# A hybrid decoder trunk on one core: eight row tiles instead of four in seven-product form for the first pair of the first MLP product in two of its four groups

## The chip, the cores and the metric

One core of a Trainium2 chip runs the whole program. The metric is the device time of one execution in microseconds; the runs of the kernel before gave 1497.21 to 1497.78 us, with a median of 1497.4 us over three. All inputs and the output are float32. Names of engines are those of the profile: PE multiplies matrices (PEld loads its weights), DVE is the vector engine, ACT the scalar engine, POOL the engine for general work, SP the engine that only issues transfers here.

## What is computed

One decoder layer on 256 tokens with 2048 channels, and 16 meta tokens ahead of them: two attention branches, gates, an output projection, and then the part that matters here, a squared-ReLU MLP with 8192 hidden channels:

```python
h = h + hybrid_mixer(rmsnorm(h, norm_mix_g[l]), ...)
h = h + squared_relu_mlp(rmsnorm(h, norm_mlp_g[l]), w_ff1[l], w_ff2[l])
return rmsnorm(h, final_norm_g)[:, N_META:]

def squared_relu_mlp(xn, w1, w2):
    return jnp.square(jax.nn.relu(xn @ w1)) @ w2
```

## The kernel before, in words

**Float32 in three products.** A float32 product is made of three products of rounded halves. Every weight tile comes from DRAM into one of five `raw` buffers (SP issues the load), ACT copies it rounded into the high half of a `w` buffer, and DVE writes the rest, `raw - high`, into the low half (`cut`, lines 967 to 975). There are five `w` buffers, too. `product_into` (line 984) then multiplies, for two row tiles: high by high, high by low, low by high, so six matmuls of 512 columns for a product, all on line 993.

**Seven products for eight.** For a pair of column blocks (`f1`, `f2 = f1 + 4`) and the two halves of the tokens, four row tiles can be taken as 2 x 2 blocks in a form with seven products instead of eight (`pair_of`, lines 998 to 1114). The form needs differences of weight tiles (`less`, on DVE, line 977) and sums of token tiles (`summed`, from the tiles given as `sums`). The steps `m1` to `m7` are its products, `held` loads the two tiles of `f2` into buffers of their own (`hb`, `hc` for the first four row tiles, `hd`, `he` for the next four; `he` lies in a tile whose name in the trace is `sums`). Row tiles outside the form are taken plainly (`plain`): one cut for twelve matmuls. `pair_of` gets a list `sums`; its length `nq` says how many fours of row tiles take the form. With `nq == 1` the form has eight steps, 42 matmuls and 7 cuts, 4 differences, and twelve plain steps follow (`rest`). With `nq == 2` it has sixteen steps, 84 matmuls, 14 cuts, 8 differences, and eight plain steps follow; the tile of `f1` then stays in its `raw` buffer, is overwritten there with a difference (`got["a", q]`), and one tile of `f2` is loaded a second time (`m3`).

**The MLP.** The 8192 hidden channels are taken in four groups (`NG`). A group has four pairs: two of the first product (operand `x2`), two of the second (operand `a`, made by `hidden` from the first product's results). The loop over `coming` (lines 1363 to 1393) runs the plain steps of one pair and puts the first steps of the next pair between them; the tables `at` say after which plain step each goes. This document calls the four rounds of that loop in a group stage 0 to stage 3: in stage 3 the plain steps of the second product's second pair run, between the first steps of the next group's first pair. Only the second pair of the second product had `nq == 2`, with the sums tiles `s_a` and `s_x2`.

**The sums of x2.** The token sums of `x2`'s first four row tiles are made in the output projection (`token_sums`, line 907 ff., out of `gained`, line 1267), stay in `s_x2`, are stored to DRAM (`kept_sums`, line 1279) and are loaded again by four transfers on POOL's queue in stage 3 of each group (line 1378), since `s_x2` holds sums of `a` in between.

**What sets the order.** Each engine runs its instructions in one fixed order, which a scheduler makes from the program's order and the dependences; PE's order may mix the matmuls of several steps.

Of the kernel before, what the change touches and what calls it, by code (L numbers as in the profile page):

```python
# [7 lines left out]
F32 = mybir.dt.float32  # L8
# [4 lines left out]
ALU = mybir.AluOpType  # L13
# [3 lines left out]
P = 128  # L17
# [3 lines left out]
NT = 256  # L21
# [10 lines left out]
RAW = 5  # L32
NL = 4
SUMS_AT = 24
SX_AT = 0
PARTS_AT = 56

# [36 lines left out]
def trunk(ctx: ExitStack, tc: tile.TileContext, hT, w_small, w_all, consts, w_alpha2, out):  # L74
    nc = tc.nc
    serial = [0]

    def nm(s):
        serial[0] += 1
        return f"{s}_{serial[0]}"  # L80
# [5 lines left out]
    dram = ctx.enter_context(tc.tile_pool(name="dram", bufs=1, space=bass.MemoryType.DRAM))  # L86
# [93 lines left out]
    def gemm2(w, x, k0=0, nk=KT, pool=None, last=None):  # L180

        ps = bank(pool or pg, "ps")
        for k in range(nk):
            hi, lo = w(k0 + k)
            if last is None or k < nk - 1:
                mac2(ps, hi, lo, x[:, k], k == 0, k == nk - 1)
            else:
                nc.tensor.matmul(steps(ps), hi, steps(row(x[:, k])), start=False, stop=False)
                nc.tensor.matmul(steps(ps[:, 0:NT]), lo, steps(last), start=False, stop=True)
        issued()  # L190
        return ps
# [51 lines left out]
    def total(ps, t=None):  # L243

        b = tmp.tile([P, NT], F32, tag="evb", name=nm("evb"), bufs=1)
        nc.scalar.copy(b, ps[:, NT:512])
        if t is None:
            t = sums4[:, NT * (turns[0] % 4) : NT * (turns[0] % 4 + 1)]
            turns[0] += 1
        nc.vector.tensor_tensor(t, ps[:, 0:NT], b, op=ALU.add)  # L250
        return t

    def split_to(dst_hi, dst_lo, src):
        nc.scalar.copy(dst_hi, src)
        nc.vector.tensor_tensor(dst_lo, src, dst_hi.bitcast(F32), op=ALU.subtract)
# [44 lines left out]
    def operand(pool, name, nk=KT, at=0, **kw):  # L300

        t = pool.tile([P, at + nk * 2 * NT], F32R, name=nm(name), **kw)
        return t[:, at:].rearrange("p (k o t) -> p k o t", o=2, t=NT)
# [33 lines left out]
    def gain(i, k):  # L337
        return residual[0][:, k, NA + i : NA + i + 1]
# [59 lines left out]
    for s in range(KT // 2):  # L398
# [5 lines left out]
        for kk in range(2):  # L404
            k = 2 * s + kk
# [496 lines left out]
    def token_sums(dst, src, temp):  # L902

        v = temp.rearrange("p (s k m) -> p s k m", s=4, m=P)
        c, d = (v[:, i].rearrange("p k (c r) -> p k c r", r=32) for i in (0, 1))
        s3, s4 = (v[:, i].rearrange("p k (c r) -> p k c r", r=32) for i in (2, 3))
        nc.vector.tensor_tensor(c, src(0, 1), src(1, 1), op=ALU.add)
        nc.vector.tensor_tensor(s3, src(0, 0), src(0, 1), op=ALU.subtract)
        nc.vector.tensor_tensor(d, c, src(0, 0), op=ALU.subtract)
        nc.vector.tensor_tensor(s4, src(1, 0), d, op=ALU.subtract)  # L910
        split_to(dst[:, :, :, 0, :], dst[:, :, :, 1, :], v)
# [13 lines left out]
    for t in range(2):  # L925
        nc.sync.dma_start(line1[:, P * t : P * t + P], rbt[0:1, P * t : P * t + P])
        nc.sync.dma_start(r1[:, t : t + 1], line1[:, P * t : P * t + P].rearrange("o p -> p o"))
    s_x = keep.tile([P, 32 * P + 64], F32R, tag="h", name="s_x")[:, SX_AT : SX_AT + 32 * P].rearrange(
        "p (q s k o m) -> p q s k o m", q=2, k=2, o=2, m=P)
# [245 lines left out]
    for j0 in (12, 14):  # L1175
# [4 lines left out]
        for j in range(2):  # L1180
            t = total(gemm2(w, of, k0=8 * j, nk=8))
            nc.vector.tensor_tensor(gates[2 * j], gates[2 * j], t, op=ALU.mult)
        for j in range(2):
            t = total(gemm2(next_weights(), og))
# [13 lines left out]
    ht = residual[0][:, :, NM:NA]  # L1198
    x2 = operand(keep, "x2", at=24, tag="s2")
# [18 lines left out]
    def turn_tile():  # L1218
        return gat.tile([P, KT * P], F32, tag="o", name=nm("turn"))

    def sums_tile(name):
        t = fp.tile([P, 16 * P + 64], F32R, name=name)
        return t[:, SUMS_AT : SUMS_AT + 16 * P].rearrange("p (s k o m) -> p s k o m", k=2, o=2, m=P)

    s_x2, s_a = sums_tile("s_x2"), sums_tile("s_a")
    gained = turn_tile()
    kept = dram.tile([P, KT * NT], F32, name="kept")
    kept_sums = dram.tile([P, 16 * P], F32, name="kept_sums").rearrange("p (s k o m) -> p s k o m", k=2, o=2, m=P)

    a_box = {}  # L1230

# [5 lines left out]
    def pairs():  # L1237
        for g in range(NG):
            for p in range(2):
                yield (g, p), lambda: pair_of(blocks(), x2, [s_x2], lambda f, pt, g=g, p=p: hidden(  # L1240
                    operand_a(g), 2 * p + f, pt, None if p else s_a if f == 0 else s_x2 if g < NG - 1 else None,
                    (g, p, f) == (NG - 1, 1, 1)), p == 0)
            for p in range(1 if g == NG - 1 else 2):
                yield None, lambda: pair_of(blocks(), operand_a(g), [s_a, s_x2] if p else [s_a], lambda f, pt, g=g, p=p: gathered(g, 2 * p + f, pt), p == 0, p == 0)
# [5 lines left out]
    def blocks():  # L1250
        ff[0] += 8
        return ff[0] - 8
# [7 lines left out]
    for j in range(KT):  # L1260
        add_residual(j, gemm2(next_weights(out=True), y))
        nc.scalar.activation(x2[:, j, 0, :], ht[:, j, :], AF.Identity, scale=gain(1, j))
        nc.vector.scalar_tensor_tensor(x2[:, j, 1, :], ht[:, j, :], gain(1, j),
                                       x2[:, j, 0, :].bitcast(F32), op0=ALU.mult, op1=ALU.subtract)
        square_sum(acc2, j, j == 0)
        if j < 4:
            nc.vector.tensor_scalar(gained[:, NT * j : NT * (j + 1)], ht[:, j, :], gain(1, j), None, op0=ALU.mult)
        if j == 3:
            g4 = gained[:, 0 : 4 * NT].rearrange("p (j t c r) -> p j t c r", j=4, t=2, r=32)
            token_sums(s_x2, lambda i, t: g4[:, 2 * i : 2 * i + 2, t], gained[:, 4 * NT :])  # L1270
        if j == 3:
            tc.keep_in_program_order(nc.scalar.preload_act_table_set("natural_log_exp_and_others"))
            steps_now, rest_now = first_pair[1]()
        if j in (3, 5, 8, 11):
            for step in {3: slice(0, 1), 5: slice(1, 3), 8: slice(3, 5), 11: slice(5, 7)}[j], :
                for run in steps_now[step]:
                    run()
        if j == 8:
            nc.scalar.dma_start(kept_sums, s_x2.bitcast(F32))
        if j % 4 == 3:  # L1280
            nc.scalar.dma_start(kept[:, NT * (j - 3) : NT * (j + 1)].rearrange("p (j t) -> p j t", t=NT),
                                ht[:, j - 3 : j + 1, :])
# [25 lines left out]
    def hidden(a, b, pt, sums, last):  # L1308

        both = turn_tile()  # L1310
        u = both[:, 4 * NT :].rearrange("p (t f) -> p t f", t=2)

        def part(t):
            nc.scalar.activation(u[:, t, :], pt[t], AF.Relu, scale=r2[:, t : t + 1])
            nc.scalar.activation(u[:, t, :], u[:, t, :], AF.Square)
            return cells(u[:, t, :])

        def ready(back):
            turned_parts(a, b, back)
            if b == 0:  # L1320
                summed(back)
            elif sums is not None:
                behind.append([2, lambda: summed(back)])

        def summed(back):
            token_sums(sums, lambda i, t: back[:, 2 * i : 2 * i + 2, t], both[:, 0 : 8 * P])

        turn([lambda t=t: part(t) for t in range(2)], ready, both, slots=(6, 9, 11) if last else (7, 11, 14 if b == 0 else 15))
# [34 lines left out]
    index, late = 0, []  # L1363
    while rest_now:
        key, make = next(coming, (None, None))
        steps_next, rest_next = make() if make else ([], [])
        at = {1: (0, 3, 4, 5, 6, 8, 9, 10), 2: (0, 2, 1, 2, 4, 5, 5, 6, 7, 7, 8, 8, 9, 9, 10, 11),
              3: (0, 2, 4, 5, 5, 6, 6, 7)}.get(index % 4, (0, 2, 3, 4, 5, 7, 9, 10))
        if index == 0:
            steps_now[7]()  # L1370
        closing = index == 4 * NG - 3
        for i, run in enumerate(rest_now):
            run()
            if index == 0 and i == 2:
                norm2()
            if index % 4 == 3 and i == 0:
                for q in range(4):
                    nc.gpsimd.dma_start(s_x2[:, q].bitcast(F32), kept_sums[:, q])
            for n, step in enumerate(steps_next):
                if at[n] == i and closing and n > 4:  # L1380
                    late.append(step)
                elif at[n] == i:
                    step()
            if not steps_next and i in (1, 3, 5):
                late.pop(0)()
        issued()
        rest_now, index = rest_next, index + 1
# [169 lines left out]
```

## Time and profile before

| | before |
|---|---|
| runs, median (lowest to highest) | 1497.4 us (1497.21 to 1497.78), three runs |
| the profiled execution | 1497.08 us; its span, first to last instruction, 1495.1 us; granted clock 0.999 |
| PE busy | 1484.9 us, 99% of the span |
| DVE busy | 1193.2 us, 80% |
| ACT busy | 878.4 us, 59% |
| POOL busy | 119.8 us, 8% |
| moved by DMA | 335.00 MB, 224 GB/s over the span |
| PE's share of the chain that ended last | 96% |

PE is busy from one end to the other; what DVE, ACT and the transfers do lies beside it. The share of DVE is a mean over stages: in some of them it has far less room than 80% says, and a reader should look at each stage by itself.

### The profile page before, as it was taken

What the parts mean: (1) busy time and instruction counts of PE and PEld (TensorE: products, weight loads), DVE (VectorE), ACT (ScalarE), POOL (GpSimd) and SP (SyncE); (2) the same over time, 40 slices, a digit from 0 to 9 for tenths busy, and PEclk for the clock granted to TensorE, in tenths of its full rate; (3) what the DMA queues carried; (4) which work ended last, traced back from release to release, by engine and by line L of the source; (5) the groups of instructions that cost most, each with busy time, mean ns of one, the idle gap of its engine ahead of it and who ended that gap; (6) DMA issues with size and microseconds to landing.
All of it is one profiled execution on the core that took longest, in us unless ns stands there. A gap on an engine that the chain in (4) does not pass through costs nothing.

```text
span 1495.1 us, 22541 instructions
## 1 busy us (share of the span) xinstructions
PE 1484.9 (99%) x8374; PEld 1322.2 (88%) x8374; DVE 1193.2 (80%) x1578; ACT 878.4 (59%) x1246; POOL 119.8 (8%) x202
## 2 busy tenths in 40 slices
PE   9999999999999999999999999999999999999997
PEld 8999999999999888888988888888888888888887
DVE  7899858586677877876788889877998889898766
ACT  7765444455555555555566666666665566556645
POOL 6012100111111000000011100000000000000004
PEclk9999999999999999999999999999999999999999
DMA  9545555465547677678678678877777778888783
GB/s 325 176 145 185 182 170 180 159 213 170 169 163 247 212 224 233 205 230 286 223 248 253 204 248 264 267 230 242 250 244 249 230 250 252 266 260 273 249 277 110
DMA packets 242545, 335.00 MB, mean 224 GB/s; under 512 B 13130, under 2 KB 209748, under 8 KB 242180
## 3 DMA queue, kind: packets, MB, share of 16 engines
q1 hardware_dynamic: 219940, 299.22, 61.2%
q10 hardware_dynamic: 21360, 30.09, 6.5%
q0 software_dynamic: 1136, 4.27, 0.9%
q8 instruction: 65, 1.06, 0.3%
q14 instruction: 44, 0.36, 0.1%
HBM read 316.22 MB, written 17.31 MB: 223 GB/s over the span
## 4 chain that ended last, share of the span: by engine, by line
PE 96%; DVE 2%; issue 1%; ACT 1%; POOL 0%; POOLq 0%; DVEq 0%; ACTq 0%
PE bx L993 17%; PE ps L169 14%; PE bv L993 11%; PE by L993 11%; PE bz L993 11%; PE ps L170 7%; PE psa L174 5%; PE psa L178 5%; PE psa L176 4%; PE gla L993 4%; PE fox L993 2%; PE ps L429 1%; PE ps L431 1%; PE ps L1424 1%; DVE w L135 1%
## 5 line engine op out<-in xcount | busy, mean ns | idle before, releaser
L973 DVE TENSOR_TENSOR w<-raw,w 128x1024 fp32r<-128x1024 f32 x300 | 365.4, 1224 | 100.9 <-ACT w L972 96.6
L972 ACT CAST w<-raw 128x1024 fp32r<-128x1024 f32 x300 | 312.3, 1048 | 203.6 <-PE bx L993 68.2
L135 DVE TENSOR_TENSOR w<-raw,w 128x1024 fp32r<-128x1024 f32 x198 | 243.0, 1229 | 81.5 <-ACT w L134 80.1
L134 ACT CAST w<-raw 128x1024 fp32r<-128x1024 f32 x198 | 207.4, 1049 | 92.4 <-PE psa L178 30.3
L169 PE MATMUL ps<-x,w 128*128 128x512 f32 x543 | 184.4, 383 | 0.0
L174 PE MATMUL psa<-x,w 128*128 128x272 f32 x640 | 181.7, 285 | 0.0
L178 PE MATMUL psa<-x,w 128*128 128x272 f32 x640 | 179.6, 282 | 0.0
L176 PE MATMUL psa<-x,w 128*128 128x272 f32 x624 | 175.9, 282 | 0.0
L170 PE MATMUL ps<-x,w 128*128 128x256 f32 x543 | 149.0, 274 | 0.0
L993 PE MATMUL bx<-w,x 128*128 128x512 f32 x528 | 131.1, 381 | 0.0
L174 PEld LDWEIGHTS psa<-x,w 128*128 128x128 f32 x640 | 120.2, 188 | 0.2
L178 PEld LDWEIGHTS psa<-x,w 128*128 128x128 f32 x640 | 120.2, 188 | 0.1
L176 PEld LDWEIGHTS psa<-x,w 128*128 128x128 f32 x624 | 117.4, 188 | 0.0
L169 PEld LDWEIGHTS ps<-x,w 128*128 128x128 f32 x543 | 101.9, 188 | 17.1
L993 PEld LDWEIGHTS bx<-w,x 128*128 128x128 f32 x528 | 98.8, 188 | 17.4
L993 PE MATMUL by<-w,x 128*128 128x512 f32 x444 | 112.5, 381 | 0.0
L170 PEld LDWEIGHTS ps<-x,w 128*128 128x128 f32 x543 | 102.0, 188 | 0.0
L993 PEld LDWEIGHTS by<-w,x 128*128 128x128 f32 x444 | 83.2, 188 | 14.6
L993 PE MATMUL bv<-w,x 128*128 128x512 f32 x360 | 91.9, 381 | 0.0
L993 PE MATMUL bz<-w,x 128*128 128x512 f32 x360 | 91.6, 381 | 0.0
L169 PE MATMUL ps<-y,w 128*128 128x512 f32 x256 | 85.6, 380 | 0.0
L993 PE MATMUL bx<-w,a 128*128 128x512 f32 x336 | 83.7, 380 | 0.0
(405 smaller groups left out, 2741.1 us busy)
## 6 DMA issues: line engine op xcount, KB each, us to landing
raw<-w_all_dram SPq DMA_DIRECT2D x489, 512.0 KB, 4.6
there<-turn ACTq DMA_DIRECT2D x80, 128.0 KB, 3.9
turn<-there ACTq DMA_DIRECT2D x20, 512.0 KB, 4.7
hb<-w_all_dram SPq DMA_DIRECT2D x18, 512.0 KB, 4.4
hc<-w_all_dram SPq DMA_DIRECT2D x18, 512.0 KB, 5.3
raw<-w_all_dram SPq DMA_DIRECT2D x26, 256.0 KB, 5.0
raw<-w_all_dram SPq DMA_DIRECT2D x8, 384.0 KB, 6.8
hd<-w_all_dram SPq DMA_DIRECT2D x6, 512.0 KB, 7.1
```

The costliest lines, as they stand in the source:

```text
L134: copied = nc.scalar.copy(hi[:, k, :], r).ins
L135: return copied, nc.vector.tensor_tensor(lo[:, k, :], r, hi[:, k, :].bitcast(F32), op=ALU.subtract).ins
L169: nc.tensor.matmul(steps(ps), hi, steps(row(x)), start=first, stop=False)
L170: nc.tensor.matmul(steps(ps[:, 0:NT]), lo, steps(x[:, 0, :]), start=False, stop=last)
L174: nc.tensor.matmul(steps(ps[:, X_LO]), hi, steps(x_lo[:, k]), start=first, stop=False, skip_group_check=True)
L176: nc.tensor.matmul(steps(ps[:, 0:NA]), lo, steps(x_hi[:, k]), start=False, stop=last and hi is None, skip_group_check=True)
L178: nc.tensor.matmul(steps(ps[:, 0:NA]), hi, steps(x_hi[:, k]), start=False, stop=last, skip_group_check=True)
L429: nc.tensor.matmul(steps(ps), hi, steps(row(x[:, k])), start=st, stop=False)
L431: nc.tensor.matmul(steps(ps[:, 0:NT]), lo, steps(x[:, k, 0]), start=False, stop=sp)
L972: copied = nc.scalar.copy(hi, r).ins
L973: made(copied, nc.vector.tensor_tensor(lo, r, hi.bitcast(F32), op=ALU.subtract).ins, 1)
L993: nc.tensor.matmul(steps(ps), l, steps(r), start=start and k == 0 and i == 0, stop=False, skip_group_check=True)
```

## The change

In groups two and three (`TWO = (1, 2)`) the first pair of the first product gets `[s_x2, s_a]` instead of `[s_x2]`, so `nq == 2` there. For that, the output projection also makes the token sums of `x2`'s row tiles 4 to 7 (into `s_a`), stores them to a second DRAM tile, and stage 3 of groups one and two loads both. The tables of places follow: sixteen first steps between the eight plain steps of stage 3, and in stage 0 of groups two and three, which now has eight plain steps, the eight first steps of the next pair one after each.

```diff
+TWO = (1, 2)
...
-    kept_sums = dram.tile([P, 16 * P], F32, name="kept_sums").rearrange("p (s k o m) -> p s k o m", k=2, o=2, m=P)
+    kept_sums = [dram.tile([P, 16 * P], F32, name=n).rearrange("p (s k o m) -> p s k o m", k=2, o=2, m=P)
+                 for n in ("kept_sums", "kept_sums2")]
...
-                yield (g, p), lambda: pair_of(blocks(), x2, [s_x2], lambda f, pt, g=g, p=p: hidden(
+                yield (g, p), lambda: pair_of(blocks(), x2, [s_x2, s_a] if p == 0 and g in TWO else [s_x2], lambda f, pt, g=g, p=p: hidden(
...
-        if j < 4:
-            nc.vector.tensor_scalar(gained[:, NT * j : NT * (j + 1)], ht[:, j, :], gain(1, j), None, op0=ALU.mult)
-        if j == 3:
+        if j == 4:
+            gained = turn_tile()
+        if j < 8:
+            nc.vector.tensor_scalar(gained[:, NT * (j % 4) : NT * (j % 4 + 1)], ht[:, j, :], gain(1, j), None, op0=ALU.mult)
+        if j in (3, 9):
...
-            token_sums(s_x2, lambda i, t: g4[:, 2 * i : 2 * i + 2, t], gained[:, 4 * NT :])
+            token_sums(s_x2 if j == 3 else s_a, lambda i, t: g4[:, 2 * i : 2 * i + 2, t], gained[:, 4 * NT :])
...
-        if j == 8:
-            nc.scalar.dma_start(kept_sums, s_x2.bitcast(F32))
+        if j in (8, 13):
+            nc.scalar.dma_start(kept_sums[j // 13], (s_x2 if j == 8 else s_a).bitcast(F32))
...
-              3: (0, 2, 4, 5, 5, 6, 6, 7)}.get(index % 4, (0, 2, 3, 4, 5, 7, 9, 10))
+              3: (0, 1, 1, 3, 2, 3, 4, 4, 5, 5, 5, 6, 6, 6, 7, 7) if len(steps_next) > 8 else (0, 2, 4, 5, 5, 6, 6, 7),
+              }.get(index % 4, (0, 2, 3, 4, 5, 7, 9, 10) if len(rest_now) > 8 else (0, 1, 2, 3, 4, 5, 6, 7))
...
-                    nc.gpsimd.dma_start(s_x2[:, q].bitcast(F32), kept_sums[:, q])
+                    for tile_of, kept_of in list(zip((s_x2, s_a), kept_sums))[0 : len(steps_next) // 8]:
+                        nc.gpsimd.dma_start(tile_of[:, q].bitcast(F32), kept_of[:, q])
```

**DVE at the start of stage 3 of group one, before.** The names `w_...` are the cuts' halves in program order; `raw`, `hb`, `hc`, `hd` and `sums` are what they or the differences (L977) read.

```order
L973 TENSOR_TENSOR w_9870<-raw_9868,w_9870 128x1024
L973 TENSOR_TENSOR w_9895<-raw_9893,w_9895 128x1024
L973 TENSOR_TENSOR w_9912<-raw_9910,w_9912 128x1024
L973 TENSOR_TENSOR w_9929<-raw_9927,w_9929 128x1024
L977 TENSOR_TENSOR hd_9932<-hb_9889,raw_9927 128x1024
L973 TENSOR_TENSOR w_9945<-raw_9943,w_9945 128x1024
L973 TENSOR_TENSOR w_9964<-raw_9962,w_9964 128x1024
L973 TENSOR_TENSOR w_9979<-hd_9932,w_9979 128x1024
L977 TENSOR_TENSOR hd_9932<-hc_9891,hd_9932 128x1024
```

The same place in the changed program, three cuts further on:

```order
L974 TENSOR_TENSOR w_9932<-raw_9930,w_9932 128x1024
L978 TENSOR_TENSOR raw_9930<-hb_9906,raw_9930 128x1024
L974 TENSOR_TENSOR w_9945<-raw_9943,w_9945 128x1024
L974 TENSOR_TENSOR w_9962<-raw_9960,w_9962 128x1024
L978 TENSOR_TENSOR raw_9960<-hd_9927,raw_9960 128x1024
L974 TENSOR_TENSOR w_9976<-raw_9974,w_9976 128x1024
L974 TENSOR_TENSOR w_9993<-raw_9930,w_9993 128x1024
L978 TENSOR_TENSOR hb_9906<-hc_9908,hb_9906 128x1024
L974 TENSOR_TENSOR w_10005<-raw_9960,w_10005 128x1024
L978 TENSOR_TENSOR hd_9927<-sums_78,hd_9927 128x1024
L978 TENSOR_TENSOR hc_9908<-hc_9908,raw_9930 128x1024
L974 TENSOR_TENSOR w_10020<-raw_10018,w_10020 128x1024
```

The differences come twice as often, three of them lie between the cuts `w_9993` and `w_10020`, and two `raw` buffers (9930 and 9960) stay in use from their load to differences at the end of these rows and just behind them.

**PE at the same place, before** (`by`, `bx`, `bz`, `bv` are accumulators):

```order
L993 MATMUL by_9622<-w_9870,a_8986 128x4x32x4 x6
L993 MATMUL bx_9529<-w_9870,a_8986 128x4x32x4 x6
L993 MATMUL by_9622<-w_9895,a_8986 128x4x32x4 x6
L993 MATMUL bx_9529<-w_9895,a_8986 128x4x32x4 x6
L993 MATMUL by_9622<-w_9912,a_8986 128x4x32x4 x6
L993 MATMUL bx_9529<-w_9912,a_8986 128x4x32x4 x6
L993 MATMUL bx_9934<-w_9929,x_1064_7876 128x4x32x4 x6
```

And in the changed program, from `w_9976` to `w_10035`:

```order
L994 MATMUL by_9635<-w_9976,a_8999 128x4x32x4 x6
L994 MATMUL bx_9542<-w_9976,a_8999 128x4x32x4 x6
L994 MATMUL bz_9703<-w_10020,a_8999 128x4x32x4
L994 MATMUL bv_9578<-w_10020,a_8999 128x4x32x4
L994 MATMUL bv_9998<-w_9993,s_x_7880 128x4x32x4 x6
L994 MATMUL bv_9998<-w_10005,s_a 128x4x32x4 x6
L994 MATMUL bx_9936<-w_10035,s_x_7880 128x4x32x4
L994 MATMUL bz_9703<-w_10020,a_8999 128x4x32x4 x5
L994 MATMUL bv_9578<-w_10020,a_8999 128x4x32x4 x5
L994 MATMUL bx_9936<-w_10035,s_x_7880 128x4x32x4 x5
```

Plain products (twelve matmuls to a cut) give way to products of the form (six to a cut), and PE takes the first matmul of a product, which needs the high half alone, ahead of other products.

**DVE in the output projection, before**, after the sums of the first four row tiles (`s_x`):

```order
L255 TENSOR_TENSOR s_x_7880<-turn_7882,s_x_7880 128x8x128
L135 TENSOR_TENSOR w_8249<-raw_8248,w_8249 128x1024
L1263 SCALAR_TENSOR_TENSOR x_1064_7876<-h_7397,x_1064_7876 128x256
L1212 TENSOR_TENSOR h_7397<-ps_8172,h_7397 128x256
L135 TENSOR_TENSOR w_8296<-raw_8295,w_8296 128x1024
L1213 TENSOR_TENSOR h_7397<-h_7397,evb_8205 128x256
L135 TENSOR_TENSOR w_8301<-raw_8300,w_8301 128x1024
```

The same place in the changed program:

```order
L256 TENSOR_TENSOR s_x_7880<-turn_7882,s_x_7880 128x8x128
L1271 TENSOR_SCALAR turn_8163<-h_7397 128x256
L136 TENSOR_TENSOR w_8253<-raw_8252,w_8253 128x1024
L1265 SCALAR_TENSOR_TENSOR x_1064_7876<-h_7397,x_1064_7876 128x256
L1213 TENSOR_TENSOR h_7397<-ps_8175,h_7397 128x256
L136 TENSOR_TENSOR w_8301<-raw_8300,w_8301 128x1024
L1214 TENSOR_TENSOR h_7397<-h_7397,evb_8208 128x256
L136 TENSOR_TENSOR w_8306<-raw_8305,w_8306 128x1024
```

Four such scalings, four narrow sums and one 1024-wide subtraction are put between the cuts of this stretch.

## Rows read from the trace of the kernel before

**Rows 1.** The page: engines over the whole span, and PE's granted clock in 40 slices.

```profile
PE 1484.9 (99%) x8374; PEld 1322.2 (88%) x8374; DVE 1193.2 (80%) x1578; ACT 878.4 (59%) x1246; POOL 119.8 (8%) x202
PEclk9999999999999999999999999999999999999999
```

**Rows 2.** Busy time by stretch: group one's stages 2, 3; later stages 0, 2, 3, 0.

```profile
core 0: us, PE busy (x) PEld busy (x) DVE busy (x) ACT busy (x) POOL busy (x), PEclk, DMA share, GB/s
...
922.80:972.60 49.80, 49.80 (x228) 42.47 (x228) 43.22 (x41) 31.80 (x38) 1.68 (x3) 1.00 0.84 259
972.60:1002.70 30.10, 30.10 (x138) 25.70 (x137) 23.67 (x21) 18.69 (x22) 0.54 (x1) 1.00 0.69 224
1002.70:1043.40 40.70, 40.70 (x186) 34.73 (x185) 30.53 (x28) 24.73 (x28) 0.00 (x0) 1.00 0.75 243
...
1084.00:1133.80 49.80, 49.80 (x228) 42.51 (x227) 45.15 (x44) 30.88 (x35) 1.62 (x3) 1.00 0.83 258
1133.80:1163.90 30.10, 30.10 (x138) 25.68 (x138) 25.76 (x26) 16.57 (x17) 0.54 (x1) 1.00 0.70 229
1163.90:1204.60 40.70, 40.70 (x187) 34.73 (x186) 31.23 (x30) 23.75 (x26) 0.00 (x0) 1.00 0.74 240
```

**Rows 3.** The chain that ended last, stage 3 of group one: start, us, what.

```profile
972.96 1.32 PE by L993 x6
974.28 1.32 PE bx L993 x6
```

**Rows 4.** Timeline, around the ends of stage 2 of groups one and two.

```profile
964.11 3.53 DVE L973 TENSOR_TENSOR w<-raw,w 128x1024 fp32r<-128x1024 f32 x3 [0.69 <-ACT w L972]
...
965.34 1.05 ACT L972 CAST w<-raw 128x1024 fp32r<-128x1024 f32 x1 [0.27 <-PE by L993]
...
972.80 1.48 PE L993 MATMUL by<-w,a 128*128 128x512 f32 x6
...
1126.75 3.49 DVE L973 TENSOR_TENSOR w<-raw,w 128x1024 fp32r<-128x1024 f32 x3
...
1134.05 0.69 DVE L1338 TENSOR_TENSOR h<-bz,h 128x512 f32<-128x512 f32 x1
...
1135.15 1.04 PE L993 MATMUL by<-w,a 128*128 128x512 f32 x4
```

**Rows 5.** DVE's cuts of raw, 922.8 to 1204.6 us: busy, mean ns, idle before them.

```profile
L973 DVE TENSOR_TENSOR w<-raw,w 128x1024 fp32r<-128x1024 f32 x101 | 122.5, 1221 | 31.9 <-ACT w L972 31.0
```

**Rows 6.** The busiest stretch for transfers, and raw's landing times in it.

```profile
1325.10:1365.70 40.60, 40.60 (x186) 34.65 (x185) 35.23 (x36) 23.40 (x26) 0.00 (x0) 1.00 0.95 306
DMA to landing us min/median/max: 3.2/5.1/6.3
```

**Rows 7.** The tile kept_sums: its loads on POOL's queue, landing times of all its transfers.

```profile
L1378 POOL DMA_DIRECT2D s_x<-kept_sums x12: 538/538/602, 944.2 to 1298.0; - x12
L1279 ACTq DMA_DIRECT2D kept_sums<-s_x x1: 338/338/338, 778.6 to 778.6; - x1
DMA to landing us min/median/max: 4.1/4.6/6.2
```

**Rows 8.** Output projection: DVE's instructions that the change repeats, and a cut with PE's use.

```profile
758.99 0.35 DVE L1267 TENSOR_SCALAR turn<-h 128x256 f32<-128x256 f32 x1
...
761.58 0.83 DVE L1267 TENSOR_SCALAR turn<-h 128x256 f32<-128x256 f32 x1
...
762.72 0.41 DVE L908 TENSOR_TENSOR turn<-turn 128x256 f32<-128x256 f32 x1
...
777.39 1.22 DVE L255 TENSOR_TENSOR s_x<-turn,s_x 128x1024 fp32r<-128x1024 f32 x1
778.53 1.22 DVE L135 TENSOR_TENSOR w<-raw,w 128x1024 fp32r<-128x1024 f32 x1
...
781.76 0.38 PE L169 MATMUL ps<-y,w 128*128 128x512 f32 x1
```

**Rows 9.** Busy time in a stretch of the output projection, columns as in rows 2.

```profile
780.00:820.00 40.00, 40.00 (x232) 35.81 (x231) 36.91 (x45) 25.97 (x40) 7.31 (x8) 1.00 0.83 266
```

## The prediction

> **What bounds the kernel now.** [...] So the question is what the change does to PE's work, and whether PE still gets it in time. Next I cut the MLP into the stages of its loop and read the busy time of each [rows 2]: the reader should see that PE's busy time equals the length of every stretch, so PE never waits there, and that DVE is at 87 to 91% in stage 2 (43.22 of 49.8 us, 45.15 of 49.8 us) and lower in stages 3 and 0. Then the chain of waits: in stage 3 it is PE alone, six matmuls in 1.32 us [rows 3]. Last the timeline, for how far DVE is ahead: at the end of stage 2 of group one the third of three cuts ends at 964.11 + 3.53 = 967.64 us and PE starts on it at 972.80 us, a lead of 5.2 us; in group two 1126.75 + 3.49 = 1130.24 and 1135.15 us, a lead of 4.9 us [rows 4]. That lead is what the change may use up.
>
> **What goes: twelve matmuls.** A form on four row tiles takes 7 x 6 = 42 matmuls where plain steps take 4 x 12 = 48. One form more in two groups saves 12 matmuls of 512 columns. One costs 1.32 / 6 = 0.22 us [rows 3], so **2.64 us** less work on PE. [...] The rows say 0.22 us, and I go by them.
>
> **What comes in stage 3 of groups one and two.** PE's work there grows from 138 to 180 matmuls (39.6 us), with 22 cuts instead of 15 and 8 differences instead of 4. A cut or difference in a row of three costs DVE 3.53 / 3 = 1.18 us [rows 4]. Eleven more are 13.0 us: DVE has 23.67 + 13.0 = 36.7 us in group one and 25.76 + 13.0 = 38.7 us in group two [rows 2], of 39.6 us. That is 93% and 98%, more than any stage has now, but under PE's own time by 2.9 and 0.9 us. ACT gets seven casts of 1.05 us [rows 4], 18.69 + 7.4 = 26.0 us of 39.6: no bound.
>
> Totals don't say when PE needs a cut, so I counted both engines' orders at the densest place. From the cut `w_9993` to `w_10020` DVE has five instructions, three of them differences: 5.9 us. PE needs the low half of `w_9993` at its second matmul and that of `w_10020` only after the rest of `w_9993` (5), `w_10005` (6) and one of `w_10035`, since the order lets it start the plain product with the high half: 12 matmuls, 2.6 us. The lead falls by 3.3 us there. In group two the two adds into `h`, 0.69 us each [rows 4], come in close behind and make it 4.7 us. The lead before that place is capped by the five `w` buffers: the cast for `w_9993` can start when PE is through with the cut five earlier, 38 matmuls before its first one, so 39 before the low half is needed (8.6 us), less 0.27 us of signal, 1.05 us of cast [rows 4] and 1.22 us of subtraction [rows 5]: 6.0 us. So 2.7 us should be left in group one and 1.3 us in group two, and PE should not wait. If each cut is also held up as long as cuts are today, 31.9 / 101 = 0.32 us [rows 5], PE waits somewhat; that is the first rival. Taken: 0.2 us over both stages.
>
> **What leaves stage 0 of groups two and three.** 186 matmuls become 138 (30.4 us) and four cuts go: DVE has 30.53 - 4.7 = 25.8 us and 31.23 - 4.7 = 26.5 us [rows 2], 85 to 87%. No wait is expected; cost 0. Its cover is the 4 us of spare DVE time, and without it `hidden`'s transposes would be late.
>
> **Transfers.** Stage 3 now asks for 18 weight tiles of 512 KB (ten for the form, since two are loaded twice) and eight slices of sums of 256 KB: 11.5 MB in 39.6 us, 291 GB/s, where it had 224 and 229 GB/s [rows 2]. Against a worry stands the stretch at 1325 us: 306 GB/s for 40.6 us, and PE busy without a break, raw's loads landing after 5.1 us in the median and 6.3 us at most [rows 6]. Taken: 0. POOL's queue issues eight loads where it issued four, in each of two stages, the slice of `s_a` ahead of that of `s_x2`. Each waits until the older sums have been read; the one before landed in 4.1 to 6.2 us [rows 7], and the first is issued at 944.2 us [rows 7], some 40 us before the first product that reads the sums. Behind them POOL has nothing until the last group, and nobody waits: 0. Without that cover the form's fourth product would wait up to 6.2 us.
>
> **The output projection.** DVE gets four scalings of 0.35 to 0.83 us, four narrow adds of 0.41 us and one subtraction of 1.22 us [rows 8], so 4.3 to 6.2 us; ACT gets a cast of 1.05 us and one issue of 0.34 us [rows 4, 7]. From 780 to 820 us DVE has 40 - 36.91 = 3.1 us free [rows 9], and the tightest cut, 778.53 + 1.22 = 779.75 us, is used at 781.76 us, a lead of 2.0 us [rows 8]. Only one scaling (0.83 us at most) has come in ahead of that cut. Bounds: 0, if all fits in free time and lead, to 6.2 - 3.1 - 2.0 = 1.1 us of waiting. I take 0, since the later additions are spread over five row tiles.
>
> **Sum.** The profiled execution took 1497.08 us. 1497.08 - 2.64 + 0.2 + 0 = 1494.6 us; the median of the runs, 1497.4 us, lies 0.3 us above it, so I forecast **1495.0 us**, 0.16% faster. A measurement of this kernel can tell about 0.2% (3.0 us) from no change, so the whole gain stays just under that bound.
>
> **Rivals.**
> *One, held-up cuts give part of it back.* With 0.32 us of wait per cut, 22 cuts cost 7.0 us: in group one 36.7 + 7.0 = 43.7 us, 4.1 us over PE's time, which the lead of 5.2 us covers; in group two 45.7 us, 6.1 over, 1.2 us more than its lead of 4.9 us. With the output projection at its bound that is 2.3 us of waiting, so -0.3 us, 1497.1 us; without it 1495.9 us. For it: DVE at 98%. Against it: today's waits arise mostly because DVE is ahead and ACT waits for PE to free a buffer; they go when DVE is late.
> *Two, slower: loads come late, since two of the five `raw` buffers are held* by `got["a"]` until the differences are made. Three buffers turn over in landing, cast and subtraction, 5.1 + 1.05 + 1.22 = 7.4 us [rows 4 to 6], which is 3 x 0.524 MB / 7.4 us = 213 GB/s for `raw`. If the stage is served at 229 GB/s, as now [rows 2], 11.5 MB take 50.2 us, 10.6 more than PE needs; less the lead of 5 us that is 5.6 us in each of two stages, 11.2 - 2.6 = +8.6 us, 1506 us. It decides from the point where each stage waits over 2.8 us (then the time is 3.0 us above today's), that is where the 11.5 MB take over 47.4 us, under 243 GB/s. For it: the form holds these buffers for some 15 us. Against it: four of the eighteen loads go to buffers of their own, some of them already in stage 2, and stage 2 holds `raw` in the same way and runs at 258 and 259 GB/s with PE full [rows 2].
> *Three, more than the products go.* A gain over 3.0 us needs 0.4 us beside the 2.64; no row shows PE waiting in these stages, so only the scatter of runs (0.6 us between the lowest and the highest) could give it.
> [...]
> That the change doesn't do what it says is excluded by the order: PE has twelve matmuls fewer.
>
> **Chances and range.** The forecast, all but at most 1 us of the gain kept (1494.4 to 1495.8 us): 0.65. Rival one (1495.8 to 1499 us): 0.17. Rival two (over 1500.4 us): 0.08. Rival three: 0.09. Rival four: 0.01. Faster by over 0.2% is rival three, 0.09; slower by over 0.2% is rival two, 0.08; the rest, 0.83, lies within. The range from 1494.4 to 1497.8 us leaves out rival three below and, above, rival two and the upper end of rival one (about 0.03).
>
> **What would show it.** Right: line 994 has twelve matmuls fewer in the program, PE stays full in both stages 3, which are about 39.6 us long, DVE is at 92% or more in them, stage 0 of groups two and three is 30 us long, and `s_a`'s loads on POOL are no one's wait. Rival one would show as gaps of PE behind DVE's cuts in stage 3 of group two; rival two as ACT's casts waiting for `raw` transfers, and as a stage with DMA share near 1 or with SP waiting for the differences. I am wrong if PE waits over 1 us in either stage 3 or in the output projection, or if the time falls below 1494.4 us.

## The result, and the profile of the changed kernel

| | before | changed |
|---|---|---|
| runs, median (lowest to highest) | 1497.48 us (1497.21 to 1497.78), six runs | 1503.18 us (1500.94 to 1504.6), six runs |
| ratio, 95% interval | | 1.0036 [1.0024, 1.0047]: slower, by 0.36% |
| the profiled execution; its span | 1497.08 us; 1495.1 us | 1500.94 us; 1499.0 us |

The prediction was 1495.0 us, in 1494.4 to 1497.8 us. The changed kernel is 5.7 us slower in the median instead of 2.5 us faster, and its runs scatter by 3.7 us where those of before scatter by 0.6. The profile shown is of the fastest of its runs. Two far slower executions, of 2180.64 and 3969.45 us among the runs of the first two experiments below, are left out of every median and range here.

The page of the changed kernel, engines, PE's granted clock, and the chain by engine (compare [rows 1]):

```profile
PE 1486.2 (99%) x8362; PEld 1319.7 (88%) x8362; DVE 1209.0 (81%) x1601; ACT 881.1 (59%) x1253; POOL 125.7 (8%) x210
...
PEclk9999999999999999999999999999999999999999
...
PE 93%; DVE 4%; ACT 1%; issue 1%; DMA 0%; POOL 0%; ACTq 0%; POOLq 0%; DVEq 0%
```

PE has twelve matmuls fewer, 8362 for 8374, and yet it is busy for 1.3 us longer, at the same granted clock (0.999 in both traces). So something is wrong with the time of a matmul, not only with waits. Busy time by stage (columns as in [rows 2]; the last two rows are stretches of equal length before and behind 1245 us):

```profile
972.60:1012.20 39.60, 39.60 (x182) 33.79 (x181) 34.31 (x32) 25.71 (x30) 0.54 (x1) 1.00 0.68 219
1012.20:1042.60 30.40, 30.40 (x140) 25.94 (x139) 25.93 (x25) 19.88 (x24) 0.00 (x0) 1.00 0.85 271
1042.60:1083.20 40.60, 39.48 (x177) 32.60 (x176) 33.83 (x40) 24.75 (x32) 0.00 (x0) 1.00 0.68 229
...
1133.00:1172.60 39.60, 39.60 (x180) 33.31 (x179) 36.90 (x35) 23.77 (x25) 0.54 (x1) 1.00 0.70 227
1172.60:1203.00 30.40, 30.40 (x139) 25.55 (x138) 27.11 (x27) 18.51 (x22) 0.00 (x0) 1.00 0.79 258
1203.00:1243.60 40.60, 40.60 (x184) 34.02 (x183) 33.19 (x39) 25.08 (x32) 0.00 (x0) 1.00 0.76 246
...
780.00:820.00 40.00, 40.00 (x233) 35.81 (x232) 39.30 (x53) 27.15 (x42) 8.86 (x9) 1.00 0.83 284
1084.00:1244.00 160.00, 160.00 (x720) 134.44 (x719) 143.12 (x146) 97.77 (x113) 4.29 (x8) 1.00 0.79 256
1248.00:1408.00 160.00, 160.00 (x729) 136.53 (x728) 141.13 (x144) 98.61 (x113) 2.15 (x4) 1.00 0.83 266
```

PE is full in both stages 3 (first and fourth row), in both stages 0 (second and fifth) and in the output projection. It is not in stage 1 of group two, 1042.6 to 1083.2 us: 39.48 of 40.6 us, 177 matmuls where 186 had run. And there is a second loss that PE's busy share does not show: with PE at 160.00 of 160 us, 720 matmuls start between 1084 and 1244 us, and 729 between 1248 and 1408 us (PEld, the weight loads, is busy for 134.44 and 136.53 us). From one start to the next it takes 0.2227 us in the mean there instead of 0.2200.

The waits of PE, changed kernel (waited for: us in total, times, longest):

```profile
PE bx L994 <- ACT w L973: 1.6, 2, 0.9
...
PE bz L994 <- ACT w L973: 0.9, 2, 0.5
```

So casts on ACT are late. The timeline of ACT and DVE in stage 1 of group two says why, at two places (start, us, what; in brackets idle time before it and what ended it):

```profile
1050.06 0.42 DVE L911 TENSOR_TENSOR turn<-turn 128x256 f32<-128x256 f32 x1
...
1050.51 1.05 ACT L255 CAST s_a<-turn 128x1024 fp32r<-128x1024 f32 x1 [3.24 <-DVE turn L911]
1051.59 1.23 DVE L256 TENSOR_TENSOR s_a<-turn,s_a 128x1024 fp32r<-128x1024 f32 x1 [1.11 <-ACT s_a L255]
1052.74 1.22 DVE L978 TENSOR_TENSOR hd<-hb,raw 128x1024 f32<-128x1024 f32 x1
1054.04 1.05 ACT L973 CAST w<-hd 128x1024 fp32r<-128x1024 f32 x1 [2.48 <-DVE hd L978]
...
1076.13 0.43 DVE L911 TENSOR_TENSOR turn<-turn 128x256 f32<-128x256 f32 x1
1076.59 1.05 ACT L255 CAST s_x<-turn 128x1024 fp32r<-128x1024 f32 x1 [4.32 <-DVE turn L911]
1077.68 1.23 DVE L256 TENSOR_TENSOR s_x<-turn,s_x 128x1024 fp32r<-128x1024 f32 x1 [1.12 <-ACT s_x L255]
...
1078.82 1.22 DVE L978 TENSOR_TENSOR hd<-raw,hd 128x1024 f32<-128x1024 f32 x1
...
1080.15 1.05 ACT L973 CAST w<-hd 128x1024 fp32r<-128x1024 f32 x1 [2.50 <-DVE hd L978]
...
1081.10 3.89 ACT L973 CAST w<-raw 128x1024 fp32r<-128x1024 f32 x4
...
1081.24 0.49 PE L994 MATMUL bx<-w,a 128*128 128x512 f32 x1 [0.67 <-ACT w L973]
...
1082.19 0.49 PE L994 MATMUL bz<-w,x 128*128 128x512 f32 x1 [0.46 <-ACT w L973]
```

The first place in the kernel before, where the same difference stands ahead of the sums' cast:

```profile
1047.20 1.22 DVE L977 TENSOR_TENSOR hd<-hb,raw 128x1024 f32<-128x1024 f32 x1
...
1048.79 1.05 ACT L254 CAST s_a<-turn 128x1024 fp32r<-128x1024 f32 x1 [0.83 <-DVE turn L910]
```

Read the first five rows of the changed kernel as a relay. DVE ends the last narrow add of `a`'s token sums (L911); ACT, idle for 3.24 us, casts the sums; DVE, idle for 1.11 us, subtracts them; only then comes the difference `hd` (L978), which in the kernel before comes 1.6 us ahead of the cast of `s_a`; and ACT, idle for 2.48 us, gets its next weight cast. In ACT's order casts of tiles stand behind that of `hd`: at the second place four of them run one after another from 1081.10 us on, in 3.89 us, behind the cast of `hd` at 1080.15 us. Between 1047.3 and 1054.0 us ACT makes no weight cast at all, and with that DVE's lead falls from 4.7 us (the cut before it ends at 1050.14, PE starts on it at 1054.83 us) to 0.2 us at 1057.5 us. At the second place the same relay takes the rest, and PE waits. In group three it repeats, around 1241 to 1247 us.

**Where 3.9 us came from.** Summing what each start of a matmul lies behind the one before, over 0.22 us: 0.26 us around 1063 us, 1.66 us at 1081 to 1082.5 us, 1.89 us at 1246 to 1247.5 us, 3.8 us of waits in all (the list of waits shows 2.5 us of them, as it leaves out the time in which the matmul before still counts as busy). From the first of them to 1245 us the mean spacing is 223.3 and then 222.7 ns instead of 220.0, about 800 matmuls, 2.3 us. With 2.64 us less to do and 0.2 us in the first 22 us of the program: 3.8 + 2.3 - 2.6 + 0.2 = 3.7 us; the other 0.2 us lie behind the last matmul.

In the program's order the suspect is one position. `hidden` stores relu's square turned to DRAM, loads it back, and puts the rest on when a count of cuts has gone by (`slots`, in `turn`): after 14 cuts for the pair's first result (`a` and its sums `s_a`), after 15 and 2 more for the second (sums `s_x`). A cut that fills the count puts them on at once, inside `cut`. Stage 0 of groups two and three has fewer cuts now, so the 14th is that of `m1` and the 17th that of `m2`, two steps of the next form that go on with a difference. `less` (L978) keeps that difference in the program's order, and in the trace it stands behind the subtraction of the sums, which was put on just before it. Before, the counts ran out one cut earlier for `s_a` and one later for `s_x`, at cuts of plain steps.

### The profile page after: what moved, and what is told of

Its sections match the earlier page's. It is cut to its first block, busy times and chain, and to the rows that moved or that the text cites. A ratio compares the mean times of both kernels' runs of the same rounds, so it can differ in the third digit from the quotient of the medians.

```text
span 1499.0 us, 22594 instructions
## 1 busy us (share of the span) xinstructions
PE 1486.2 (99%) x8362; PEld 1319.7 (88%) x8362; DVE 1209.0 (81%) x1601; ACT 881.1 (59%) x1253; POOL 125.7 (8%) x210
## 3 DMA queue, kind: packets, MB, share of 16 engines
q0 software_dynamic: 1776, 6.37, 1.3%
## 4 chain that ended last, share of the span: by engine, by line
PE 93%; DVE 4%; ACT 1%; issue 1%; DMA 0%; POOL 0%; ACTq 0%; POOLq 0%; DVEq 0%
PE bx L994 17%; PE ps L170 14%; PE by L994 10%; PE bv L994 10%; PE bz L994 9%; PE ps L171 7%; PE psa L175 4%; PE psa L179 4%; PE gla L994 4%; PE psa L177 4%; PE fox L994 2%; PE ps L430 1%; PE ps L432 1%; PE ps L1430 1%; DVE w L974 1%
## 5 line engine op out<-in xcount | busy, mean ns | idle before, releaser
L994 PE MATMUL bz<-w,x 128*128 128x512 f32 x336 | 88.5, 383 | 0.9 <-ACT w L973 0.9
L994 PE MATMUL bv<-w,x 128*128 128x512 f32 x336 | 88.2, 382 | 0.0
```

The source lines that it names most:

```text
L994: nc.tensor.matmul(steps(ps), l, steps(r), start=start and k == 0 and i == 0, stop=False, skip_group_check=True)
```

## The experiments

Theory A: this order is the cause. Rival B: stage 0, 10 us shorter, leaves the round trip and DVE too little time wherever the sums are put. Rival C: the second sums' loads or the held `raw` buffers. Runs of before beside these have medians of 1497.37 to 1497.63 us and reach from 1496.69 to 1502.36 us; every ratio is to them, with its 95% interval, and need not be that of the medians.

**Both sums one cut earlier** (changed kernel):

```diff
-        turn([lambda t=t: part(t) for t in range(2)], ready, both, slots=(6, 9, 11) if last else (7, 11, 14 if b == 0 else 15))
+        turn([lambda t=t: part(t) for t in range(2)], ready, both, slots=(6, 9, 11) if last else (7, 11, (13 if moved else 14) if b == 0 else (14 if moved and b == 1 else 15)))
```

`moved` is true in groups two and three.

> Theory A (order): in the changed kernel the token sums of a (four narrow adds, a cast on ACT, a subtraction on DVE) are put on directly behind the cut of a step whose difference `less` must follow them in the program's order, so DVE makes hd only behind the subtraction, ACT's cast of hd waits for that, and the casts behind it too; the lead of the cuts is lost twice in stage 1 of groups two and three. Here both sums are put on one cut earlier, ahead of another step. A expects the gain of the twelve matmuls to come through: 1494.4 to 1495.4 us, runs within 1 us of each other, PE without a gap from 1040 to 1250 us. Rival B (time): stage 0 is 10 us shorter, so the round trip through DRAM and DVE's work in stage 1 come too late wherever the sums are put: 1500 to 1504 us, gaps in stage 1 as now. Rival C (transfers): the second sums' loads or the held raw buffers delay the cuts: 1500 to 1504 us as well.

Measured: 1495.62 us in the median of ten runs, 0.9991 [0.9982, 0.9999]; seven lie from 1495.2 to 1495.8 us, three from 1497.1 to 1497.85 us. Its timeline at the first place, and its windows:

```profile
1049.76 1.22 DVE L978 TENSOR_TENSOR hd<-hb,raw 128x1024 f32<-128x1024 f32 x1
...
1051.07 1.05 ACT L973 CAST w<-hd 128x1024 fp32r<-128x1024 f32 x1 [1.75 <-DVE hd L978]
...
1052.97 1.04 ACT L255 CAST s_a<-turn 128x1024 fp32r<-128x1024 f32 x1
```

```profile
1042.60:1083.20 40.60, 40.60 (x186) 34.65 (x185) 37.73 (x44) 28.43 (x35) 0.00 (x0) 1.00 0.85 263
...
1084.00:1244.00 160.00, 160.00 (x729) 136.51 (x728) 146.26 (x148) 101.25 (x115) 4.29 (x8) 1.00 0.83 260
```

The difference now comes 3.2 us ahead of the sums' cast, though the sums are put on earlier in the program. So, as these traces have it, the difference is held back by what is put on between its own cut and itself, not by all that was put on before. PE is full, and 729 matmuls start in 160 us. From 802 us to the last matmul this execution gains exactly 2.64 us on the one of before; 0.65 us of it were lost ahead of 22 us, where the other ten traces lose 0.15 to 0.66 us, and 0.26 us behind the last matmul. So the medians differ by 1.75 us only, and the median lies 0.2 us above A's range. The three slower runs, which A did not expect, have no profile; the kernel before has such runs as well, so their cause is open. B and C fall as the cause of the loss: stage 0 is as short, and the loads are the same.

**The kernel before, with its sums put on those steps:** the same line of the kernel before, for groups two and three with 15 for 14 and 14 for 15 (so `s_x` comes one cut earlier, not two as the expectation has it).

> The kernel before with its twelve plain steps in stage 0, where in groups two and three the sums are put on so that they fall on the very steps on which they fall in the changed kernel (s_a one cut later, s_x two cuts earlier). Theory A: the kernel before gets slower by this alone, 1499 to 1503.5 us, with the lead lost in stage 1 of groups two and three and gaps of PE near the second place. Rival B and rival C: nothing is shortened and nothing loaded, so 1497.3 to 1497.8 us.

Measured: 1502.29 us in the median of five runs, 1501.83 to 1508.63 us, 1.0043 [1.0029, 1.0056]. The profile is of the slowest of them. Second place, and windows (here and below: us, PE busy and matmuls, granted clock, DMA share, GB/s):

```profile
1077.13 1.05 ACT L254 CAST s_x<-turn 128x1024 fp32r<-128x1024 f32 x1 [3.32 <-DVE turn L910]
...
1080.68 1.05 ACT L972 CAST w<-hd 128x1024 fp32r<-128x1024 f32 x1 [2.50 <-DVE hd L977]
```

```profile
900.00:1060.00 160.00, 160.00 (x729) 1.00 0.77 243
1084.00:1244.00 160.00, 160.00 (x702) 1.00 0.75 236
```

The order alone, without any other part of the change, makes the kernel before about as slow as the changed one: A stands. But PE waits only 1.7 us in this trace, and its span is 11 us longer than before. Nearly all of the rest is spacing: 702 matmuls in 160 us, 0.2283 us from start to start, with no wait of PE in those 160 us.

**One of the two alone** (changed kernel: 13 and 15; 14 and 14).

> Changed kernel, only the sums s_a one cut earlier; s_x's stay on the step with the difference. Theory A: the cuts come to the second place with a lead of 4 to 5 us instead of 0.2 to 0.9, and ACT's standstill of some 7 us there costs at most 1 us a group: 1495 to 1497.5 us. If the second place alone is enough, 1499 us or more. Rivals B and C: 1500 to 1504 us.

> Changed kernel, only the sums s_x one cut earlier; s_a's stay on the step with the difference. Theory A: the lead falls to about 0.2 us at the first place, where PE lost 0.3 us at most, and then comes back slowly: 1495 to 1498 us; if PE's slower spacing (222.7 ns for 220.0 ns from the first small gap at 1063 us on) starts with that small gap, 2 to 3 us more, 1497 to 1500.5 us. Rivals B and C: 1500 to 1504 us.

Measured: with `s_a` earlier 1500.92 us, 1.0019 [1.001, 1.0027]; with `s_x` earlier 1503.09 us, 1.0052 [1.0034, 1.007], runs from 1501.65 to 1509.72 us. Either place alone is enough to make the kernel slower than before, which A as I had put it did not expect; the second lies in the range of B and C, which the first experiment had ruled out. In the trace with `s_x` earlier (the run of 1501.65 us) PE waits 0.26 us around 1064 us, and from there to 1440 us the mean spacing is 223.3 ns. The waits of PE from 845 to 1440 us, and two windows, with only `s_a` earlier:

```profile
PE bz L994 <- ACT w L973: 0.2, 1, 0.2
```

```profile
900.00:1060.00 160.00, 160.00 (x729) 1.00 0.82 263
1090.00:1250.00 160.00, 160.00 (x718) 1.00 0.81 257
```

The one wait in the list is late, at 1323 us. Yet from 1080 us on the mean spacing is 223.3 ns: around 1080 us a few matmuls started up to 14 ns late, 0.05 us in all, and the pace did not come back. So the length of a wait does not look like its price. Theory D: any wait can shift PE into a slower steady spacing. Rival E: the spacing is that of cuts that come just in time.

**One short wait, nothing else** (both sums earlier; `plain`, one cut in stage 1 of group two, where the lead is 6.7 us):

```diff
+            plains[0] += 1
+            if plains[0] == 79:
+                part = w[1][:, 0, 0:16].bitcast(F32)
+                tc.keep_in_program_order(nc.gpsimd.tensor_copy(w[1][:, 0, 0:16], part))
+                for _ in range(7):
+                    tc.keep_in_program_order(nc.gpsimd.memset(holder("he"), 0.0))
+                tc.keep_in_program_order(nc.gpsimd.tensor_copy(w[1][:, 0, 0:16], part))
```

> The version with both sums one cut earlier (no wait of PE in the MLP, 1495.4 us), plus one wait of PE and nothing else: in stage 1 of group two, POOL rewrites 16 columns of the low half of one plain cut with their own values after seven fills of an idle buffer (0.95 us each by the trace), so that PE gets this half some 0.5 us (0 to 1.2) after it wants it; ACT, DVE and the transfers have no more to do. Theory D (rhythm): a wait of any length can put PE's matmuls into a slower even spacing (220.0 ns to 222.7, 223.3 or 228.3 ns as in the profiles seen), which stays until the next wait: some 1800 matmuls follow in the MLP, so the wait itself plus 4.9, 5.9 or 15 us, 1500 to 1511 us, and runs that scatter by several us; or, where the rhythm happens to stay at 220.0, only the wait. Rival E (late cuts): the slower spacing in the changed kernel comes from cuts that arrive just in time; here the cuts are ahead by 2 us or more, so only the wait itself: 1495.5 to 1496.6 us, and 220.0 ns behind it.

> Control to the one short wait: the same, with five fills instead of seven, so POOL is through some 1.4 us before PE wants the half. Both theories: 1495.2 to 1495.8 us, PE without a gap from 850 to 1440 us and 220.0 ns. If the fills on POOL or the rewritten columns cost something by themselves it shows here.

Measured: the control, with five fills, 1495.38 us, 0.9988 [0.9979, 0.9996], nine of its ten runs up to 1496.06 us and one at 1499.87; the one wait 1501.84 us, 1.0034 [1.0018, 1.005], its runs in three clusters: one at 1495.19, eight from 1501.0 to 1502.7, three from 1510.2 to 1510.4 us. The profile is of one at 1510 us, PE around the wait, and POOL's last write of the half:

```profile
1046.97 1.48 PE L994 MATMUL bx<-w,x 128*128 128x512 f32 x6
1048.29 0.38 PE L994 MATMUL by<-w,x 128*128 128x512 f32 x1
...
1048.73 0.39 PE L994 MATMUL bx<-w,a 128*128 128x512 f32 x1
1048.76 0.36 POOL L1033 CAST w<-w 128x16 fp32r<-128x16 f32 x1
...
1049.18 0.99 PEld L994 LDWEIGHTS by<-w,x 128*128 128x128 f32 x5 [0.47 <-POOL w L1033]
1049.18 1.41 PE L994 MATMUL by<-w,x 128*128 128x512 f32 x5
...
1051.57 1.53 PE L994 MATMUL by<-w,x 128*128 128x512 f32 x6
1052.94 1.30 PE L994 MATMUL bx<-w,x 128*128 128x512 f32 x5
```

```profile
880.00:1040.00 160.00, 160.00 (x729) 1.00 0.80 254
1060.00:1220.00 160.00, 160.00 (x702) 1.00 0.79 253
1240.00:1400.00 160.00, 160.00 (x702) 1.00 0.80 251
```

Six matmuls take 1048.29 - 1046.97 = 1.32 us ahead of the wait and 1052.94 - 1051.57 = 1.37 us behind it. The weight loads stand idle until POOL's write ends, at 1049.12 us, and PE goes on 0.06 us behind it; the wait itself is 0.45 - 0.22 = 0.23 us. Some (1440 - 1049.2) / 0.22 = 1776 matmuls of 512 columns follow: by 8.3 ns they cost 14.8 us, by 3.3 ns 5.9 us, by none 0, and 1495.4 us plus these and the wait are about the three clusters. D stands, and E falls as the reason for the slower spacing: the cuts lead by 6.7 us here. Only one run has a profile, so the spacing of the two lower clusters is inferred from their times, and whether PE waited at all in the run of 1495.19 us is not shown.

**A way back?** In each trace the narrow matmuls of the output projection are followed by 220.0 ns. So with the one wait every tenth product of the MLP took its last matmul as two of 256 columns; and, in the three-group version below, the products ahead of the output projection did, where every trace has 222.7 ns:

```diff
+                halves = [slice(0, 512)]
+                if k + i == 3:
+                    products[0] += 1
+                    if products[1] and products[0] % products[1] == 0:
+                        halves = [slice(0, 256), slice(256, 512)]
...
+                    for c in halves:
```

> The kernel with one short wait, and in the whole MLP every tenth product (every sixtieth matmul, some 13 us apart) takes its last matmul as two of 256 columns, which give the same sums. The stretch that mixes 512 and 256 columns at the end of the output projection is followed by 220.0 ns in every profile so far. Theory F (width): a narrow matmul lets the weight loads catch up, so the rhythm is back at 220.0 ns by the next split: 1495.5 to 1497 us with little scatter. Theory G (the rhythm is drawn again at each disturbance and a narrow matmul is only one more): 1497 to 1510 us, with the spacing changing at the splits. If splits change nothing: 1501 to 1511 us as with the one wait.

> The three-group version (1494.1 us), where the products ahead of the output projection, 505 to 690 us, which run at 222.7 ns in every profile of this study, take every tenth product's last matmul as two of 256 columns. Theory F: 220.0 ns from the first split on, some 780 matmuls by 2.7 ns, 2.1 us less: 1491.8 to 1492.6 us. Theory G, or if the 222.7 ns belong to what is multiplied there: 1494 us or more.

Measured: with the one wait 1506.27 us, 1.0056 [1.0043, 1.0068], five runs within 0.5 us; with three groups 1495.2 us, 0.9985 [0.9976, 0.9994]. The latter's ratio does not differ from that of the version without splits (0.9983), but the traces do: from the first matmul into `gla` to the last into `fox` it is 218.1 us with splits and 216.8 without. F falls. Start of the MLP with splits (the row of x7 holds one):

```profile
839.52 1.48 PE L1002 MATMUL bx<-w,x 128*128 128x512 f32 x6
840.84 1.49 PE L1002 MATMUL by<-w,x 128*128 128x512 f32 x7
842.16 1.52 PE L1002 MATMUL bx<-w,x 128*128 128x512 f32 x6
843.52 1.50 PE L1002 MATMUL by<-w,x 128*128 128x512 f32 x6
844.86 1.50 PE L1002 MATMUL bx<-w,x 128*128 128x512 f32 x6
```

Six take 1.32 us up to the split, 1.36 us just behind it and then 1.34 us: a narrow matmul is one more disturbance. In the rest of this trace the mean spacing between splits is 223.3 or 224.1 ns nearly everywhere, 233.3 ns once (1059 to 1073 us, behind the first split after the wait) and 220.0 ns twice (851 to 856 and 1075 to 1085 us). So a split can bring 220.0 ns back, but seldom does. Why these runs scatter less than those with the wait alone is open.

**The output projection's part alone** (`TWO = ()`).

> The changed kernel with TWO = (): all pairs of the first product as in the kernel before, but the token sums of row tiles 4 to 7 are made in the output projection and stored, though nothing reads them. The prediction put this part at 0 (bound 1.1 us), so 1497.2 to 1497.8 us; if the output projection carries part of the loss, 1498.5 us or more.

Measured: 1497.58 us, 1.0000 [0.9991, 1.0008]. The second token sums and their store cost nothing that these runs can tell.

**Group four as well** (both sums earlier, `TWO = (1, 2, 3)`).

> Both sums one cut earlier, and group four's first pair in the two forms as well (TWO = (1, 2, 3)). By the order theory (A) six matmuls more go, 1.32 us, if stage 3 of group three and stages 0 and 1 of group four bring no wait: 1494.0 to 1494.6 us. Rival C (transfers): stage 0 of group four moved 306 GB/s in the kernel before, and gets shorter by 10 us: if its loads come late, a wait and a slower rhythm behind it, 1496 to 1499 us.

Measured: 1494.14 us, 0.9983 [0.9975, 0.9992]; eight runs lie from 1493.65 to 1494.39 us, three from 1496.95 to 1499.22 us, without a profile. From 802 us to the last matmul its trace gains 3.96 us on the one of before, 18 matmuls by 0.22 us. Its median is under those of both kernels.

## Why the prediction was wrong

- *Twelve matmuls, 2.64 us:* right to the hundredth where nothing waits (sums one cut earlier, from 802 us on). A lower price of a matmul, which the 0.01 of rival four stood for, is shown by no run: no stretch of 24 matmuls of 512 columns has a mean spacing under 219.96 ns in any of these traces.
- *Stage 3, transfers, POOL, output projection:* right in that they cost nothing. PE is full in both stages 3, with DVE at 34.31 and 36.90 of 39.6 us, 87 and 93% (less than the 36.7 and 38.7 us I had put, against [rows 2], and in the first of the two under the 92% that I had named as a sign); transfers ran at 219 and 227 GB/s there, not 291, so not all the loads that I had put into stage 3 fell into it; the output projection measured 0 by itself. Rivals one and two had the wrong place: PE does not wait in stage 3, and the loss goes away with the same loads. By its time alone the result lies where rival two had put it (over 1500.4 us, chance 0.08); that is a coincidence, since its cause is another.
- *The step that failed:* "No wait is expected; cost 0. Its cover is the 4 us of spare DVE time", in the part on stage 0 of groups two and three. The spare time is there: DVE has 25.93 and 27.11 us of 30.4. But it covers nothing when instructions stand in the wrong order. I had worked out DVE's and PE's order at the densest place of stage 3, and not where `hidden`'s work lands once a stage loses four cuts. It moved by a cut, onto steps whose difference must follow it, and the price fell due in stage 1, where PE waited 1.9 us in group two and 1.9 us at the end of that of group three. No term of my sum covers stage 1, and the list of what would show me wrong did not name it either.
- *The second failure is of a price:* I, and each rival, took a wait of PE to cost its own length. With the one short wait, of 0.23 us in its profile, runs came out about 0, 6 or 15 us longer, since the spacing of all that follows can change. Of the changed kernel's 6.1 us of loss in this profile 3.8 are waits and 2.3 spacing. Three of its slower runs, 1502.72 to 1503.79 us, would about fit a spacing that did not return to 220.0 ns at 1247 us (some 875 matmuls more by 2.7 to 3.3 ns, 2.4 to 2.9 us); the one at 1504.6 us would need more. None of them has a profile, so that is argued, not shown.

## What to carry to other kernels

Work that is put on "after so many cuts" moves when any stage gains or loses a cut; after such a change read, in the orders of ACT and DVE, which instruction stands behind it and whether that one feeds the next cast. A kernel whose PE never waits can lose more than the length of a wait, as this one did (2.3 us of spacing beside 3.8 us of waits in the changed kernel's profile; about 0, 6 or 15 us for one wait of 0.23 us): count the matmuls started in windows of equal length, since PE's busy share can be full at a slower spacing, here 160.00 of 160 us with 729 matmuls and with 702.

## What the runs showed of the hardware that I had not expected

A stream of weight load and matmul of 512 columns ran at one of several mean spacings, all in traces with a granted clock of 0.998 or 0.999: 220.0, 222.7, 223.3 or 228.3 ns, the last seen behind a wait only, and 224.1 and 233.3 ns with split matmuls. At 220.0 ns nearly every gap is 220 ns (678 of 679 from 850 to 1000 us in most traces); at the others the gaps differ and repeat, as 225, 222, 225, 222, 225, 221 ns at 223.3. A wait of 0.23 us was enough to move it (the control without the wait stays at 220.0 ns), and in one trace it moved where a few matmuls started up to 14 ns late. It then held for up to 390 us, until the next disturbance. Behind the waits at 1246 us in the changed kernel it went back to 220.0 ns, and behind one at 1252 us in the kernel before with its sums moved it went from 228.3 to 223.3 ns. The part of the program from 507 to 680 us runs at 222.7 ns in every trace without splits, so about 2 us lie there; splitting matmuls did not get them. No stretch of 24 matmuls of 512 columns in these traces has a mean under 219.96 ns, and what sets the spacing stays open.
